# A gated-convolution and retention block on one Trainium2 core: the first head's v and gate computed plain, q and k between the quads, one convolution slice between two heads, stores on POOL's queue

## The chip, the cores and the metric

The kernel runs on one core of a Trainium2 chip. The metric is the device time of one execution, in microseconds. A core has a matrix engine (TensorE, "PE" in the profile, with its weight loads as "PEld"), a vector engine (VectorE, "DVE"), a scalar engine (ScalarE, "ACT"), a general engine (GpSimd, "POOL") and a queue engine (SyncE, "SP") from which most DMAs are issued. POOL can issue DMAs too. Each engine works through its own list of instructions in order; semaphores hold an instruction back until what it needs is there. On-chip memory has 128 partitions; matmul results go to eight accumulator banks of 128 x 512 numbers.

## The reference

One layer on x of 512 tokens by 1024 features, in float32:

```python
h    = rmsnorm(x, g_mix)
proj = h @ w_in            # conv x | B | C | q | k | v | swish gate | gate A | gate R
u    = gc * xc
y_a  = (gb * depthwise_conv3(u)) @ w_a_out
# 4 heads, q and k 256 wide with rotary, v 512 wide
ret  = retention(q, k, v, gamma_f) + retention_backward(q, k, v, gamma_b)
y_r  = (groupnorm_per_head(ret) * g_ret * silu(g_sw)) @ w_r_out
x    = x + (sigmoid(gate_a) * y_a + sigmoid(gate_r) * y_r) @ w_o
h2   = rmsnorm(x, g_ffn)
x    = x + (silu(h2 @ w_ff_gate) * (h2 @ w_ff_up)) @ w_ff_down
out  = rmsnorm(x, g_final)
```

The normalisation is a gain per feature times one number per token (1/rms), so a projection can be made from x with the gain alone, and each token's result scaled by 1/rms afterwards.

## The kernel before

Every float32 matmul is done as three matmuls of operands split into a high and a low part (`mm3`, lines 272 to 276): high times high, high times low, low times high. `split` (line 158) makes the two parts: ACT writes the high part (line 161 or 164) and DVE the low part (line 162 or 165).

Weights stream in from memory in the order of the list that `plan()` writes out (line 54). There are two kinds of entries. A "c" entry is a block of 1 MB, loaded by SP in pieces (line 198) and split into two units; `feature_major` (line 282) turns a block of 8 x 128 rows and 256 columns into two banks with features on partitions, and `token_major` (line 299) turns blocks of 4 x 128 rows and 512 columns into four banks with tokens on partitions. A "q" entry is one of seven weight forms of a Strassen product ("quad"): four quarter matrices are loaded (line 222), four of the seven forms are sums of two quarters made by DVE (line 234), and `strassen` (line 340) replaces eight products by seven. One quad yields two 512-column outputs, for example v and the swish gate of a head. Weight units are kept in five buffers, so splits run up to two and a half blocks ahead; `raw` has ten buffers for what is loaded and not yet split.

The work in order:

1. x arrives in four loads of 512 KB beside the first weight block and is split with the gain into `xu` (line 395). `SumSq` squares x (line 419), adds up, and gives 1/rms per token (`rstd_tokens`, with a pow on POOL at line 442) and as a row along the free axis (`rstd_row`).
2. `do_qk(0)` computes q and k of head 0 from the unnormalised `xu`, with 1/rms worked into the rotary table `rcs`. Then x is normalised (line 552), split into `xg`, and its four sums for Strassen are made and split (lines 567 and 569). `do_qk(1)` to `do_qk(3)` follow, from `xu`. Each rotates on DVE (lines 539 to 541) and splits and stores the result (`keep`, line 518) in DRAM from SP. `decays()` (line 488) makes the four decay tables.
3. Four quads give v and gate of the heads, two more the merge gates A and R. Results are stored from SP (lines 585 and 591).
4. `do_mix(s)` for four slices of the convolution: three weight blocks each, a product and a three-tap convolution on DVE, result z split and stored.
5. The retention, head by head: `load_head` reads q, k, the table, v and gate back; `do_scores` makes the decayed scores p; `split_v` splits v; `do_pv` multiplies p by v and applies the group norm (statistics on DVE at line 668, a pow on POOL at line 671, then lines 673 and 675); `do_t` transposes on DVE (line 175) and splits; `do_wr` multiplies by w_r_out. Its first head stores to `yrd` from SP (line 690), the next two add to it with accumulating DMAs from POOL (line 692), and the last adds in on-chip memory. The mixes 0 to 2 come before head 0's scores, mix 3 after them.
6. `ysum` (the sum in `yrd`), the gates `sgr` and z are loaded, in this order, from SP (line 629); then `do_wr(3)`, `do_wa`, the output projection and the feed-forward part, which the change doesn't touch.

512-column scratch tiles (`t512`, lines 152 and 153) have nine buffers, the large tiles (`big`) fourteen, and the tiles for `rcs`, the decay tables and the convolution's u two. The order of instructions on each engine is fixed when the kernel is built, by a scheduler that lets later instructions go ahead where they are ready and buffers are free.

Of the kernel before, what the change touches and what calls it, by code (L numbers as in the profile page):

```python
# [12 lines left out]
F32 = mybir.dt.float32  # L13
F32R = mybir.dt.float32r
AF = mybir.ActivationFunctionType
ALU = mybir.AluOpType
# [37 lines left out]
def plan():  # L54

    out = []  # L60

    def a(name, col):
        out.append(("c", name, 0, 8, col, 256))

    def b(name, row, nk, col, nc):
        out.append(("c", name, row, nk, col, nc))

    def quad(c0, c1):
        for name in FORMS:
            for u in (0, 2):  # L70
                out.append(("q", ("w", c0, c1), name, u, 2))

    for h in range(HEADS):
        a("w_in", C_Q + h * QK)
        a("w_in", C_K + h * QK)
    for h in range(HEADS):
        quad(C_V + h * VD, C_G + h * VD)
    for c in (0, 512):
        quad(C_GA + c, C_GR + c)
    for s in range(4):  # L80
        for c in (C_XC, C_GC, C_GB):
            a("w_in", c + s * 256)
    for h in range(HEADS):
        for c in (0, 512):
            b("w_r_out", h * VD, 4, c, 512)
    for c in (0, 512):
        for r in (0, 512):
            b("w_a_out", r, 4, c, 512)
    for r in (0, 512):
        for c in (0, 512):  # L90
            b("w_o", r, 4, c, 512)
    def f(q, *names):
        for n in names:
            out.append(("q", ("f", q), n, 0, 4))

    f(0, "b11", "b21", "b12", "b22")
    f(1, "b11", "b21")
    for q0, n in FF_PARTS:
        for q in range(max(q0, 1), q0 + n):
            f(q, "t1", "t2", "t3")  # L100
            if q + 1 < NQ:
                f(q + 1, "b11")
            f(q, "t4")
            if q + 1 < NQ:
                f(q + 1, "b21")
# [27 lines left out]
def block_kernel(ctx: ExitStack, tc: tile.TileContext, xT, xtok, wpack, wquad, cols, decs, rot, g_ffn, g_final, out):  # L133
# [21 lines left out]
    def bank():  # L155
        return psum.tile([P, 512], F32, tag="bank", name="bank")
# [121 lines left out]
    def act_pair(tiles, k, sl=slice(0, S)):  # L278
        hi, lo = tiles
        return hi[k // 4][:, k % 4, sl], lo[k // 4][:, k % 4, sl]  # L280

    def feature_major(rhs, evict, block0=0, row_first=False):

        c = Chunk()
        if row_first:
            pss = [bank(), bank()]
            for k in range(8):
                for m in range(2):
                    mm3(pss[m], c.w(k, m * P, P), act_pair(rhs, k), k == 0, k == 7)
            for m in range(2):  # L290
                evict(block0 + m, pss[m])
            return
        for m in range(2):
            ps = bank()
            for k in range(8):
                mm3(ps, c.w(k, m * P, P), act_pair(rhs, k), k == 0, k == 7)
            evict(block0 + m, ps)

    def token_major(lhs, row0, chunks, evict):

        pss = [bank() for _ in range(NB)]
        n = 4 * chunks
        for kk in range(n):
            if kk % 4 == 0:
                c = Chunk()
            for nb in range(NB):
                mm3(pss[nb], act_pair(lhs, row0 + kk, slice(nb * P, (nb + 1) * P)),
                    c.w(kk % 4, 0, 512), kk == 0, kk == n - 1)
        for nb in range(NB):
            evict(nb, pss[nb])  # L310
# [85 lines left out]
        split(xs[k // 4][:, k % 4, :], xu[0][k // 4][:, k % 4, :], xu[1][k // 4][:, k % 4, :],  # L396
              gmix[:, k:k + 1])

    def split_two(c):
        split_x(2 * c)  # L400
        split_x(2 * c + 1)
    prefetch(4, lambda c: load_x(2 * c, 2), split_two)
    rcs = misctile(D, "rcs").rearrange("p (i n) -> p i n", i=2)
    prefetch(2)
    nc.sync.dma_start(rcs, rot)
# [112 lines left out]
    def keep(dst, src):  # L518
        hi, lo = t512(F32R), t512(F32R)
        split(src, hi, lo)  # L520
        for d, t in zip(dst, (hi, lo)):
            nc.sync.dma_start(d, t.bitcast(F32))


    def do_qk(h):
        pss = []
        for j in range(2):
            feature_major(xu, lambda m, ps: pss.append(ps), row_first=h == 0 and j == 0)
            if h == 0 and j == 0:
                ss.rstd_tokens()  # L530
        if h == 0:
            nc.scalar.copy(rrow, ss.rstd_row())
            for i in range(2):
                nc.vector.tensor_tensor(out=rcs[:, i, :], in0=rcs[:, i, :], in1=rrow, op=ALU.mult)
        cos, sin = rcs[:, 0, :], rcs[:, 1, :]
        for j in range(2):
            for i, (c1, c2, op) in enumerate(((cos, sin, ALU.subtract), (sin, cos, ALU.add))):
                a, b = t512(), t512()
                nc.vector.tensor_tensor(out=a, in0=pss[2 * j], in1=c1, op=ALU.mult)  # L539
                nc.vector.tensor_tensor(out=b, in0=pss[2 * j + 1], in1=c2, op=ALU.mult)  # L540
                nc.vector.tensor_tensor(out=a, in0=a, in1=b, op=op)
                keep([t[:, 2 * j + i, :] for t in qkd[h]], a)

    rrow = t512()
    do_qk(0)

# [25 lines left out]
    xforms = {n: of(t) for n, t in sums(*(xs[i][:, :, o:o + 256] for o in (0, 256) for i in range(2))).items()}  # L572
    for n, i, o in (("a11", 0, 0), ("a12", 1, 0), ("a22", 1, 256)):
        xforms[n] = of((xg[0][i], xg[1][i]), o)
    for h in range(1, HEADS):
        do_qk(h)
    decays()


    def do_quad(left, right, func, func_left=None):  # L580
        def ev_sum(dst, o, f):
            def ev(tt, t):
                if f:
                    nc.scalar.activation(t, t, f)
                nc.sync.dma_start(dst[:, o + tt, :], t)
            return ev

        def ev21(tt, ps):
            t = t512()
            nc.scalar.activation(t, ps, func_left or AF.Copy)  # L590
            nc.sync.dma_start(left[:, 2 + tt, :], t)
        strassen(4, xforms, ev_sum(left, 0, func_left), ev21, ev_sum(right, 2, func), ev_sum(right, 0, func))

    for h in range(HEADS):
        do_quad(vd[h], sgd[h], AF.Silu)
    for j in range(2):
        do_quad(gad[j], grd[j], AF.Sigmoid, AF.Sigmoid)


    def do_mix(s):  # L600
# [84 lines left out]
    def do_wr(h, yr):  # L685
        for half in range(2):
            def ev(nb, ps):
                t = snap(ps)
                if h == 0:
                    nc.sync.dma_start(yrd[half][:, nb, :], t)  # L690
                else:
                    nc.gpsimd.dma_start(out=yrd[half][:, nb, :], in_=t, accum_op=ALU.add)

            def ev_last(nb, ps):
                t = ysum[half][:, nb, :]
                nc.vector.tensor_tensor(out=t, in0=ps, in1=t, op=ALU.add)
                nc.vector.tensor_tensor(out=t, in0=t, in1=sgr[half][:, nb, :], op=ALU.mult)
            token_major(yr, 0, 1, ev if h < HEADS - 1 else ev_last)

    do_mix(0)  # L700
    do_mix(1)
    do_mix(2)
    qk, tab, v, sg = load_head(0)
    p = do_scores(qk, tab)
    vv = split_v(v)
    do_mix(3)
    yr = None
    for h in range(HEADS):
        if h < HEADS - 1:
            nxt = load_head(h + 1)  # L710
        do_pv(p, vv, sg)
        if h < HEADS - 1:
            p = do_scores(nxt[0], nxt[1])
        if yr:
            new = do_t(h, sg)
            do_wr(h - 1, yr)
            yr = new
        else:
            yr = do_t(h, sg)
        if h < HEADS - 1:  # L720
            vv, sg = split_v(nxt[2]), nxt[3]


    ysum = [load(t) for t in yrd]
    sgr = [load(t) for t in grd]
    z = [[load(t, F32R) for t in x] for x in zd]
    do_wr(HEADS - 1, yr)
    sga = [load(t) for t in gad]
    mt = ([], [])
# [272 lines left out]
    def store(nb, scaled=()):  # L1002
# [28 lines left out]

    def ev_a(tt):
        to_y(a[tt], 2 + tt, 0, last=True)
        store(2 + tt)

    def ev_d(tt):
        to_y(d[tt], tt, 1, last=True)
        store(tt, (0,) if tt else ())
    prod_tm(n, forms["a22"], a, False, True, ev_a)
    prod_tm(n, forms["s4"], d, False, True, ev_d)  # L1040

# [64 lines left out]
```

## Time and profile before

| | |
|---|---|
| runs | 1101.33, 1101.3 and 1100.21 us; median 1101.3 us |
| the profiled execution | 1101.26 us |
| its span in the profile | 1099.5 us |
| mean granted clock of TensorE | 0.98 |
| moved by DMA | 177.11 MB, mean 161 GB/s |
| PEld busy | 898.4 us |

The profile gives the busy time of each engine, the same in forty equal slices, the chain of work that ended last, groups of instructions by line with their mean duration, and the DMA issues with the time to landing. The trace behind it can be asked who waited for whom, what an engine did in a stretch, and for the single instructions in order of time. Matmuls overlap, so PE's busy time is not a count of work: the number of matmuls in a stretch is.

### The profile page before, as it was taken

Reading aid. Unit: us, or ns where it says so; the run is one execution under the profiler, and the core shown is the slowest. Engines: PE = TensorE matmul, PEld = TensorE weight load, DVE = VectorE, ACT = ScalarE, POOL = GpSimd, SP = SyncE. Lnnn points to the kernel's source line nnn. Section 1 sums busy time; section 2 is a strip of 40 time slices with the busy share of each in tenths; the row PEclk is TensorE's granted clock in tenths of the full one; section 3 lists DMA queues with packets and bytes.
Section 4 is the critical chain, followed back from the end, with each engine's and each line's share of the span. In section 5 each row is a group of like instructions: output and inputs, shape, how many; then the busy total and the mean of one; then the engine's idle time right before and its main releaser. Section 6 shows DMA issues by size and latency. Waiting matters only on the chain.

```text
span 1099.5 us, 14236 instructions
## 1 busy us (share of the span) xinstructions
PE 1050.2 (96%) x5448; PEld 898.4 (82%) x5448; DVE 841.8 (77%) x1087; ACT 496.5 (45%) x667; POOL 51.8 (5%) x70
## 2 busy tenths in 40 slices
PE   7999799999999999993999979999999999999996
PEld 6878588888888888882888868889997999899985
DVE  7899987797684444568889844448988898979995
ACT  6434375556655232322235311235555555545653
POOL 1000000000000000000002200000001000010001
PEclk9999899999999999996999999999999999999999
DMA  9446675434546424744176596442116632472313
GB/s 341 166 138 217 220 263 216 160 140 179 192 152 213 149 105 145 268 148 169 58 268 137 124 310 271 175 141 68 59 58 177 172 104 85 122 185 95 137 20 95
DMA packets 57683, 177.11 MB, mean 161 GB/s; under 512 B 6544, under 2 KB 6544, under 8 KB 54288
## 3 DMA queue, kind: packets, MB, share of 16 engines
q1 hardware_dynamic: 52432, 166.78, 42.2%
q0 software_dynamic: 5184, 9.44, 5.7%
q8 instruction: 42, 0.69, 0.2%
q14 instruction: 25, 0.20, 0.1%
HBM read 134.51 MB, written 41.68 MB: 160 GB/s over the span
## 4 chain that ended last, share of the span: by engine, by line
PE 79%; DVE 15%; issue 2%; DMA 1%; ACT 1%; POOL 1%; SPq 0%; POOLq 0%; ACTq 0%; DVEq 0%
PE bank L330 28%; PE bank L836 20%; PE bank L274 10%; PE bank L275 10%; PE bank L276 10%; DVE big L175 3%; DVE wlo L162 2%; DVE big L162 1%; DMA big<-z 1%; DVE t L162 1%; DVE big L675 1%; DVE bnst L668 1%; DVE t L673 1%; POOL bnmv L671 1%; DVE t L539 1%
## 5 line engine op out<-in xcount | busy, mean ns | idle before, releaser
L162 DVE TENSOR_TENSOR wlo<-raw,whi 128x1024 fp32r<-128x1024 f32 (+1 forms) x272 | 323.7, 1198 | 162.1 <-ACT whi L161 160.0
L161 ACT CAST whi<-raw 128x1024 fp32r<-128x1024 f32 (+1 forms) x272 | 279.9, 1033 | 331.8 <-PE bank L276 86.5
L836 PE MATMUL bank<-xform,whi 128*128 128x256 f32 x1248 | 227.8, 284 | 0.0
L836 PEld LDWEIGHTS bank<-xform,whi 128*128 128x128 f32 x1248 | 194.8, 192 | 2.9 <-ACT t L929 1.6
L330 PE MATMUL bank<-whi,big 128*128 128x512 f32 x596 | 187.4, 390 | 0.4 <-DVE big L1026 0.3
L836 PE MATMUL bank<-xform,wlo 128*128 128x256 f32 x624 | 175.4, 283 | 0.0
L234 DVE TENSOR_TENSOR raw<-raw 128x1024 f32<-128x1024 f32 x112 | 132.7, 1199 | 2.4 <-DMA raw<-wquad 1.5
L330 PEld LDWEIGHTS bank<-whi,big 128*128 128x128 f32 x596 | 111.7, 188 | 25.6 <-ACT t L337 0.8
L274 PE MATMUL bank<-big,whi 128*128 128x512 f32 x320 | 126.8, 397 | 4.0 <-ACT big L164 4.0
L276 PE MATMUL bank<-big,wlo 128*128 128x512 f32 x320 | 126.8, 396 | 2.0 <-DVE wlo L162 2.0
L275 PE MATMUL bank<-big,whi 128*128 128x512 f32 x320 | 126.7, 396 | 0.0
L330 PE MATMUL bank<-whi,xform 128*128 128x512 f32 x384 | 122.9, 396 | 1.2 <-ACT whi L161 1.2
L836 PEld LDWEIGHTS bank<-xform,wlo 128*128 128x128 f32 x624 | 119.2, 192 | 0.0
L330 PE MATMUL bank<-wlo,big 128*128 128x512 f32 x298 | 116.0, 390 | 1.4 <-DVE wlo L162 1.4
L274 PE MATMUL bank<-whi,big 128*128 128x512 f32 x240 | 95.1, 399 | 5.6 <-DMA big<-z 5.6
L275 PE MATMUL bank<-wlo,big 128*128 128x512 f32 x240 | 94.4, 393 | 0.0
L276 PE MATMUL bank<-whi,big 128*128 128x512 f32 x240 | 92.6, 390 | 0.0
L330 PEld LDWEIGHTS bank<-whi,xform 128*128 128x128 f32 x384 | 73.3, 191 | 17.4 <-ACT whi L161 2.1
L330 PE MATMUL bank<-wlo,xform 128*128 128x512 f32 x192 | 76.4, 398 | 4.4 <-DVE wlo L162 4.4
L274 PEld LDWEIGHTS bank<-big,whi 128*128 128x128 f32 x320 | 61.3, 192 | 17.1 <-ACT big L164 4.3
L276 PEld LDWEIGHTS bank<-big,wlo 128*128 128x128 f32 x320 | 61.4, 192 | 15.3 <-DVE wlo L162 2.4
L275 PEld LDWEIGHTS bank<-big,whi 128*128 128x128 f32 x320 | 61.2, 191 | 13.3 <-DVE big L165 0.4
(145 smaller groups left out, 1180.8 us busy)
## 6 DMA issues: line engine op xcount, KB each, us to landing
raw<-wquad SPq DMA_DIRECT2D x112, 512.0 KB, 4.1
raw<-wpack SPq DMA_DIRECT2D x70, 512.0 KB, 4.4
qh<-t SPq DMA_DIRECT2D x16, 256.0 KB, 2.5
ql<-t SPq DMA_DIRECT2D x16, 256.0 KB, 2.5
big<-qh SPq DMA_DIRECT2D x4, 1024.0 KB, 7.2
big<-ql SPq DMA_DIRECT2D x4, 1024.0 KB, 8.7
v<-t SPq DMA_DIRECT2D x16, 256.0 KB, 2.5
sg<-t SPq DMA_DIRECT2D x16, 256.0 KB, 3.0
```

The costliest lines, as they stand in the source:

```text
L161: nc.scalar.copy(hi, src)
L162: nc.vector.tensor_tensor(out=lo, in0=src, in1=hi.bitcast(F32), op=ALU.subtract)
L175: nc.vector.transpose(o[:, :, :, b, :], i[:, :, :, q, :])
L234: nc.vector.tensor_tensor(out=t, in0=t, in1=raws[quad, more, u][:, 0:n], op=ALU.add)
L274: nc.tensor.matmul(ps, lh, rh, start=first, stop=False)
L275: nc.tensor.matmul(ps, lh, rl, start=False, stop=False)
L276: nc.tensor.matmul(ps, ll, rh, start=False, stop=last)
L330: nc.tensor.matmul(pss[tt], l, r[:, c], start=start and k == 0 and i == 0, stop=stop and k == n - 1 and i == 2, skip_group_check=True)
L539: nc.vector.tensor_tensor(out=a, in0=pss[2 * j], in1=c1, op=ALU.mult)
L668: nc.vector.bn_stats(st, ps)
L671: nc.gpsimd.tensor_tensor(out=mv[:, 3:4], in0=mv[:, 2:3], in1=mhalf[:, 0:1], op=ALU.pow)
L836: nc.tensor.matmul(o, l[:, c], r[:, k], start=start and s == 0 and k == 0 and i == 0, stop=stop and k == 3 and i == 2, skip_group_check=True)
```

## The change

- Head 0's v and gate are no longer made by a quad but as plain token-major products from the unnormalised `xu`, first of all; 1/rms per token scales the results on their way out of the banks (ACT). The 1/rms matmuls come before the last eighth of v's product (`before_v`), the row of 1/rms after v.
- q and k of each head come from the normalised `xg`, right behind that head's v and gate; the rotary table keeps its values. `decays()` moves behind the last gate quad. x comes in four loads of 256 KB and two of 512 KB.
- `do_mix(3)` moves from before the heads to between heads 0 and 1; head 0's scores and v split come ahead of `do_mix(2)` instead of `do_mix(3)`. In each head the next head's `split_v` comes before `do_t` instead of at the end.
- z and `sgr` are loaded before `do_wr(2)`; `ysum` is loaded from POOL's queue.
- The stores of q, k, v, gates, z and of the first `yrd` are issued from POOL instead of SP.

```diff
--- before.py
+++ after.py
@@ plan
+    for c in (C_V, C_G):
+        for r in (0, 512):
+            b("w_in", r, 4, c, 512)
     for h in range(HEADS):
+        if h:
+            quad(C_V + h * VD, C_G + h * VD)
         a("w_in", C_Q + h * QK)
         a("w_in", C_K + h * QK)
-    for h in range(HEADS):
-        quad(C_V + h * VD, C_G + h * VD)
...
-    def token_major(lhs, row0, chunks, evict):
+    def token_major(lhs, row0, chunks, evict, before=None):
...
+            if before:
+                before(kk)
...
-    prefetch(4, lambda c: load_x(2 * c, 2), split_two)
+    prefetch(4, load_x, split_x)
+    for k in (4, 6):
+        load_x(k, 2)
+    for k in range(4, 8):
+        split_x(k)
...
-            nc.sync.dma_start(d, t.bitcast(F32))
...
-    rrow = t512()
-    do_qk(0)
+            store(d, t.bitcast(F32))
+
+    def store(dst, t):
+        nc.gpsimd.dma_start(dst, t)
+
+    def before_v(kk):
+        if kk == 7:
+            rtok.append(ss.rstd_tokens())
+    rtok = []
+    for dst, func in ((vd[0], AF.Copy), (sgd[0], AF.Silu)):
+        def ev(nb, ps):
+            t = t512()
+            nc.scalar.activation(t, ps, func, scale=rtok[0][:, nb:nb + 1])
+            store(dst[:, nb, :], t)
+        token_major(xu, 0, 2, ev, None if rtok else before_v)
+        if func == AF.Copy:
+            rrow = snap(ss.rstd_row())
...
-    for h in range(1, HEADS):
-        do_qk(h)
-    decays()
+    def do_qk(h):
+        for j in range(2):
+            pss = []
+            feature_major(xg, lambda m, ps: pss.append(ps))
+            cos, sin = rcs[:, 0, :], rcs[:, 1, :]
+            for i, (c1, c2, op) in enumerate(((cos, sin, ALU.subtract), (sin, cos, ALU.add))):
+                a, b = t512(), t512()
+                nc.vector.tensor_tensor(out=a, in0=pss[0], in1=c1, op=ALU.mult)
+                nc.vector.tensor_tensor(out=b, in0=pss[1], in1=c2, op=ALU.mult)
+                nc.vector.tensor_tensor(out=a, in0=a, in1=b, op=op)
+                keep([t[:, 2 * j + i, :] for t in qkd[h]], a)
...
     for h in range(HEADS):
-        do_quad(vd[h], sgd[h], AF.Silu)
+        if h:
+            do_quad(vd[h], sgd[h], AF.Silu)
+        do_qk(h)
     for j in range(2):
         do_quad(gad[j], grd[j], AF.Sigmoid, AF.Sigmoid)
+    decays()
...
     do_mix(0)
     do_mix(1)
+    nxt = load_head(0)
+    p = do_scores(nxt[0], nxt[1])
+    vv, sg = split_v(nxt[2]), nxt[3]
     do_mix(2)
-    qk, tab, v, sg = load_head(0)
-    p = do_scores(qk, tab)
-    vv = split_v(v)
-    do_mix(3)
     yr = None
     for h in range(HEADS):
         if h < HEADS - 1:
             nxt = load_head(h + 1)
         do_pv(p, vv, sg)
+        t = sg
         if h < HEADS - 1:
             p = do_scores(nxt[0], nxt[1])
-        if yr:
-            new = do_t(h, sg)
+            vv, sg = split_v(nxt[2]), nxt[3]
+        new = do_t(h, t)
+        if h == 0:
+            do_mix(3)
+        else:
+            if h == HEADS - 1:
+                z = [[load(t, F32R) for t in x] for x in zd]
+                sgr = [load(t) for t in grd]
             do_wr(h - 1, yr)
-            yr = new
-        else:
-            yr = do_t(h, sg)
-        if h < HEADS - 1:
-            vv, sg = split_v(nxt[2]), nxt[3]
-
-    ysum = [load(t) for t in yrd]
-    sgr = [load(t) for t in grd]
-    z = [[load(t, F32R) for t in x] for x in zd]
+        yr = new
+
+    ysum = [bigtile(), bigtile()]
+    for t, d in zip(ysum, yrd):
+        nc.gpsimd.dma_start(t, d)
     do_wr(HEADS - 1, yr)
```

The stores at lines 585, 591 and 690 become calls of `store` as well, and the final output's function of that name is renamed.

More of the change, by code (lines that the diff above doesn't have):

```diff
@@ L280, in act_pair, with feature_major @@
         return hi[k // 4][:, k % 4, sl], lo[k // 4][:, k % 4, sl]
-    def feature_major(rhs, evict, block0=0, row_first=False):
+    def feature_major(rhs, evict, block0=0):
         c = Chunk()
[L285 to L292, printed above, removed]
         for m in range(2):
@@ L397, in split_x @@
               gmix[:, k:k + 1])
-    def split_two(c):
-        split_x(2 * c)
-        split_x(2 * c + 1)
-    prefetch(4, lambda c: load_x(2 * c, 2), split_two)
+    prefetch(4, load_x, split_x)
[3 more added lines that the diff above has]
+        split_x(k)
     rcs = misctile(D, "rcs").rearrange("p (i n) -> p i n", i=2)
@@ L521, in keep @@
         for d, t in zip(dst, (hi, lo)):
-            nc.sync.dma_start(d, t.bitcast(F32))
[L525 to L542, printed above, removed]
-    rrow = t512()
-    do_qk(0)
+            store(d, t.bitcast(F32))
[13 more added lines that the diff above has]
+            rrow = snap(ss.rstd_row())
     xg = quarters()
@@ L584, in ev @@
                     nc.scalar.activation(t, t, f)
-                nc.sync.dma_start(dst[:, o + tt, :], t)
+                store(dst[:, o + tt, :], t)
             return ev
@@ L590, in ev21 @@
             nc.scalar.activation(t, ps, func_left or AF.Copy)
-            nc.sync.dma_start(left[:, 2 + tt, :], t)
+            store(left[:, 2 + tt, :], t)
         strassen(4, xforms, ev_sum(left, 0, func_left), ev21, ev_sum(right, 2, func), ev_sum(right, 0, func))
     for h in range(HEADS):
-        do_quad(vd[h], sgd[h], AF.Silu)
+        if h:
+            do_quad(vd[h], sgd[h], AF.Silu)
+        do_qk(h)
     for j in range(2):
         do_quad(gad[j], grd[j], AF.Sigmoid, AF.Sigmoid)
+    decays()
     def do_mix(s):
@@ L689, in ev @@
                 if h == 0:
-                    nc.sync.dma_start(yrd[half][:, nb, :], t)
+                    store(yrd[half][:, nb, :], t)
                 else:
@@ L1000, in gain, with put @@
         nc.vector.tensor_tensor(out=yt, in0=yt, in1=gf[:, half * 512:(half + 1) * 512], op=ALU.mult)
-    def store(nb, scaled=()):
+    def put(nb, scaled=()):
         for half in (1, 0):
@@ L1033, in ev_a @@
         to_y(a[tt], 2 + tt, 0, last=True)
-        store(2 + tt)
+        put(2 + tt)
     def ev_d(tt):
         to_y(d[tt], tt, 1, last=True)
-        store(tt, (0,) if tt else ())
+        put(tt, (0,) if tt else ())
     prod_tm(n, forms["a22"], a, False, True, ev_a)
```

## The prediction

> **What bounds the kernel now.** I read the page's busy times first, then the waits of PE, then PE's busy time and matmul count stretch by stretch, then the timeline, the groups and the DMA issues at the holes.
>
> ```profile
> span 1099.5 us, 14236 instructions
> PE 1050.2 (96%) x5448; PEld 898.4 (82%) x5448; DVE 841.8 (77%) x1087; ACT 496.5 (45%) x667; POOL 51.8 (5%) x70
> PE   7999799999999999993999979999999999999996
> ```
>
> TensorE (PE) is the bound: 96% of the span, with holes near the start, near 510 us (the 3), near 650 us and at the end. The second view is who PE waited for.
>
> ```profile
> PE bank L274 <- ACT big L161: 19.0, 1, 19.0
> PE bank L330 <- DVE wlo L162: 5.8, 3, 2.8
> PE bank L274 <- DMA big<-z: 5.6, 1, 5.6
> PE bank L274 <- ACT big L164: 4.0, 1, 4.0
> PE bank L276 <- DVE wlo L162: 2.0, 1, 2.0
> ```
>
> Columns: total us, times, longest. Busy time counts a matmul as long at half clock as an idle array, so I count matmuls in stretches instead (the number behind PE's busy time; GB/s last, granted clock third from the end).
>
> ```profile
> 0.00:140.00 140.00, 125.84 (x511) 101.29 (x512) 124.91 (x190) 63.65 (x83) 5.78 (x10) 0.95 0.60 217
> 140.00:340.00 200.00, 200.00 (x884) 165.62 (x883) 155.64 (x152) 118.46 (x146) 0.00 (x0) 1.00 0.53 187
> 340.00:480.00 140.00, 140.00 (x620) 115.91 (x619) 66.10 (x88) 46.77 (x58) 0.00 (x0) 1.00 0.50 174
> 480.00:540.00 60.00, 41.00 (x170) 32.98 (x169) 48.21 (x81) 10.65 (x17) 4.36 (x8) 0.83 0.28 105
> 640.00:680.00 40.00, 34.42 (x142) 27.94 (x141) 15.96 (x21) 6.32 (x6) 0.00 (x0) 0.91 0.86 334
> 60.00:80.00 20.00, 17.98 (x72) 14.38 (x71) 20.00 (x23) 8.37 (x9) 0.88 (x1) 0.91 0.39 128
> ```
>
> From 140 to 340 us PE never stops: 884 matmuls of 512 columns in 200 us, 0.2262 us each. With that price:
> - 0 to 140: 511 less 16 warm-up and 8 two-column ones is 487, worth 110.2 us; **29.8 us lost**.
> - 480 to 540: 170, worth 38.5; **21.5 lost**.
> - 640 to 680: 142, worth 32.1; **7.9 lost**.
>
> A stop costs more than its wait: between 60 and 80 us 72 matmuls are worth 16.3, so 3.7 were lost, though the one wait there is the 2.0 on L276; the clock was 0.91 in that stretch. I call the other 1.7 us the restart.
>
> **Part 1, v and gate of head 0 plain.** The Strassen quad is 7 products of 4 k, 2 tiles, 3 matmuls: 168. Plain, two outputs of 8 k, 4 token blocks, 3 matmuls: 192. 24 more at 0.2262 is **+5.4 us**, certain.
>
> **Part 2, the first 140 us.** Now four q/k heads (DVE rotation, hi/lo split, decay tables, forms of x) stand before any quad, and DVE is the late one: 20.00 of 20 us busy in the last row above. After, v and gate (192 matmuls, 43.4 us) need from DVE only splits and the normalised x, and each later head pairs 168 + 96 matmuls = 59.7 us of PE.
>
> ```profile
> L162 DVE TENSOR_TENSOR wlo<-raw,whi 128x1024 fp32r<-128x1024 f32 x261 | 316.6, 1220 | 158.0 <-ACT whi L161 155.9 <-DMA z<-t 1.6
> L234 DVE TENSOR_TENSOR raw<-raw 128x1024 f32<-128x1024 f32 x108 | 130.2, 1218 | 2.4 <-DMA raw<-wquad 1.5
> L539 DVE TENSOR_TENSOR t<-bank,rcs 128x512 f32<-128x512 f32 x16 | 10.9, 680 | 0.0
> L552 DVE SCALAR_TENSOR_TENSOR big<-big,cols_sb,t 128x512 f32<-128x512 f32 x8 | 5.7, 737 | 0.0
> L161 ACT CAST t<-t 128x512 fp32r<-128x512 f32 x26 | 16.1, 618 | 54.3 <-DVE t L541 21.6 <-DVE t L622 18.8 <-DVE lw L478 5.6
> 6.51 1.15 ACT L419 ACTIVATE t<-big 128x512 f32<-128x512 f32 x2 [1.43 <-DMA big<-xT]
> 8.85 1.22 PE L274 MATMUL bank<-big,whi 128*128 128x512 f32 x2 [4.01 <-ACT big L164]
> 13.72 0.41 PE L276 MATMUL bank<-big,wlo 128*128 128x512 f32 x1
> 25.49 0.27 PE L436 MATMUL bank<-ones_r,t 128*128 128x2 f32 x1 [1.05 <-DVE t L162]
> 26.30 0.49 PE L274 MATMUL bank<-big,whi 128*128 128x512 f32 x1
> 26.94 1.99 POOL L442 TENSOR_TENSOR rtok<-rtokv,mhalf 128x4 f32<-128x4 f32 x1 [3.44 <-DVE lw L473]
> ```
>
> DVE per later head: 14 weight splits and 8 sums of a quad, 22 x 1.22 = 26.8; six evictions, 4.1; rotation and split, 16 x 0.68 = 10.9; four q/k weight splits, 4.9. Together 46.7 of 59.7 us, so it is hidden; without the pairing it would be a q/k head's 15.8 in 21.7 plus the forms, which is today's jam. While the gate's 96 matmuls (21.7 us) run, DVE must finish the 8 x 0.737 = 5.9, four x splits of 1.2 and four weight splits, 15.7 in all; the forms' 4 sums and 4 splits, 8 x 1.22 = 9.8, then fall under q0 and k0 (21.7 us, beside 10.9 of rotation: here DVE is tight).
>
> What remains lost: the first matmul comes at 8.85 because ACT squared the first 512 KB of x at 6.51; x now comes in blocks of 256 KB, and I take 7.5 (bounds 6.5 and 8.85). The half clock after it: the 11 matmuls before 13.72 us would take 2.5, not 4.9, so 2.4. Seven of the eight small matmuls took 0.8 (25.49 to 26.30), so 1.0. The new weak place is the joint between v and gate: the small matmuls come before the last 12 of v (2.7 us), while the pow behind them took 1.99, then a split (0.62 on ACT, 0.68 on DVE) before the two matmuls for the row of 1/rms, behind which the gate's matmuls are queued on PE. About 1.3 us late plus the restart of 1.7: 3.0 (bounds 0 and two such stops of 3.7). 7.5 + 2.4 + 1.0 + 3.0 = 13.9, so **-15.9 us** (bounds -19.9 and -10.1).
>
> **Part 3, mix(3) between heads 0 and 1, split_v before do_t.** The 19.0 wait is head 1's v split (L161 on ACT), queued behind head 0's norms, scores and transposes.
>
> ```profile
> 501.58 0.69 DVE L175 STREAM_TRANSPOSE big<-big 32x512 f32<-32x512 f32 x1
> 502.86 10.73 DVE L175 STREAM_TRANSPOSE big<-big 32x512 f32<-32x512 f32 x15
> 517.18 1.22 PE L274 MATMUL bank<-big 128*128 128x512 f32 x2 [18.96 <-ACT big L161]
> 485.00:523.00 38.00, 19.00 (x73) 14.76 (x72) 30.45 (x50) 6.92 (x10) 2.19 (x4) 0.73 0.38 144
> ```
>
> mix(3) is 3 x 48 = 144 matmuls, 32.6 us, more than the hole. But it brings DVE work: the mixes between 340 and 480 us had 66.10 us of DVE per 620 matmuls, 15.4 for 144. DVE then has 30.45 + 15.4 = 45.8 in a stretch where PE has (73 + 144) x 0.2262 = 49.1: it fits, closely. What is late next is the weight split of mix(3)'s last block, behind 11.4 us of transposes. I leave one stop of 0.9 and a restart: **-18.9 us** of 21.5 (bounds -21.5 and -11; the latter leaves a block of transposes uncovered). mix(2) takes mix(3)'s place over the split of head 0's scores, with the same 144 matmuls.
>
> **Part 4, z and gate loads ahead of do_wr(2), ysum on POOL's queue.**
>
> ```profile
> 644.79 0.33 SPq L629 DMA_DIRECT2D big<-yr  x1
> 645.21 0.86 SPq L629 DMA_DIRECT2D big<-gr  x2
> 646.16 2.23 SPq L629 DMA_DIRECT2D big<-z  x4
> big<-z SPq DMA_DIRECT2D x4, 1024.0 KB, 13.6
> ```
>
> SP's queue stood until 644.79 at the load of the sum that the accumulates write; z, queued behind, landed 13.6 us after issue. After, z issues once head 3's tiles come free, and do_wr(2) and do_wr(3) (192 matmuls, 43.4 us) cover 13.6 three times. ysum, now behind the accumulates on POOL, is read by evictions only, with four other banks free for PE. **-7.9 us** (bounds -7.9 and 0).
>
> **Part 5, stores on POOL's queue.** 32 for q/k, 16 each for v, gate and z, 16 for the two merge gates, 8 for yr: 104. SP issues none of them; the trace has no plain store on POOL, the nearest rows are its accumulates.
>
> ```profile
> L692 POOL DMA_DIRECT2D yr<-t x16 | 14.5, 1321 | 33.9 <-ACT t L337 33.9
> L946 POOL DMA_DIRECT2D ydr<-t x16 | 14.1, 965 | 204.3 <-DVE t L348 164.6 <-DVE t L356 27.4 <-DVE t L363 6.3
> yr<-t POOLq DMA_DIRECT2D x16, 256.0 KB, 7.2
> qh<-t SPq DMA_DIRECT2D x16, 256.0 KB, 2.5
> L671 POOL TENSOR_TENSOR bnmv<-bnmv,mhalf 128x1 f32<-128x1 f32 x16 | 8.7, 544 | 504.8 <-DVE bnmv L670 504.8
> ```
>
> At 0.97 to 1.32 us each POOL issues for 101 to 137 us of some 650, where it is idle now. Two things can bite: the pows of L671, for which DVE and then PE's banks wait, queue behind stores; and each store holds one of nine 512-column tiles for up to 7.2 instead of 2.5 us, so that a rotation (four tiles a pass) waits for one. A head's slack on DVE (59.7 - 46.7 = 13.0) covers four passes of 3.3 us. Earlier loads on SP could give a little back (bound -1). I take **+2 us**, nearer to nothing, since accumulates ahead of pows already occur for heads 2 and 3 without a PE stop; upper bound in the last rival.
>
> The Trainium skill ("SBUF — State Buffer", SBUF: two separate sides, and Who interferes with whom) speaks against the move: while DVE runs an operation that takes both its ports, such as an fp32 copy, GpSimd cannot write the descriptors of a DMA issued from its queue. By it stores would stall wherever DVE copies; this kernel's DVE work is nearly all tensor_tensor, which the page excludes, so by the rule the sum would not change, and no run here shows a stall of that kind.
>
> **Sum.** 5.4 - 15.9 - 18.9 - 7.9 + 2.0 = -35.3. The profiled execution took 1101.26 us, 1.8 more than its span and equal to the median of 1101.3, so **1066**.
>
> **Rivals.**
> - *The early jam stays* (chance 0.13): DVE is still the late engine because x's forms, rotation and quad 1's splits meet at its start. For it: DVE's 124.91 us of 140. Against: the first head's quad is gone with its 26.8 us. Part 2 gives nothing: 1066 + 15.9 = 1082.
> - *The hole moves behind mix(3)* (0.11): DVE's 45.8 of 49.1 cannot be packed, and pv(1) or the next weights come a transpose block late. 11.4 us less 2.6 already counted: 1066 + 9 = 1075.
> - *z is as late as before* (0.06): its loads wait for big tiles that head 3 still holds, or block the weights behind them on SP. Then the change doesn't do what it says here: 1066 + 7.9 = 1074. Against: 43 us of cover.
> - *Slower: the nine tiles run dry* (0.09). 24 passes of rotation and convolution end in two stores. If each pass waits for both to land, 7.2 + 2 x 0.97 = 9.1 us, a q/k head's four passes cost 36.6 less 13.0 of slack, 23.6; four heads 94, less 35.3: 1101 + 59 = 1160. It decides from (35.3 / 4 + 13.0) / 4 = 5.5 us of wait a pass. Against: nine tiles hold two passes, and the banks leave half a head between the pairs.
>
> **How the numbers follow.** Forecast 0.60, with its own range 1058 to 1072; rivals as given; 0.01 for losses that just eat the gain. The three milder rivals lie within 1082. All bounds at their best give 5.4 - 19.9 - 21.5 - 7.9 - 1 = -44.9, 1056; above, the early jam and some of a second rival reach 1085. Outside remain about 0.15. Faster by over 0.2% (about what a measurement of this kernel can tell from no change): 0.60 + 0.13 + 0.11 + 0.06 = 0.90; within it 0.01; slower 0.09.
>
> **What would show it.** Part 1: matmuls on PE up by 24. Part 2: no PE wait on wlo L162 between 40 and 140 us, and at most one stop near 30. Part 3: no long PE wait on a v split; instead mix(3)'s matmuls behind head 1's scores. Part 4: no PE wait for the z load. Part 5: POOL busy for 100 us or more, pows not over 1 us later. I am wrong if PE stops more than 15 us in all between 10 and 700 us, above all on splits that wait for a tile still being stored by POOL.

## The result

The changed kernel takes 1061.45 us (median of 4 runs, 1061.35 to 1061.88) against 1100.88 us (4 runs, 1100.21 to 1101.33): a ratio of 0.9643, 95% interval 0.9626 to 0.966. The forecast was 1066 us with a range of 1056 to 1085. The profiled execution of the changed kernel took 1061.37 us.

### The profile page after: what moved, and what is told of

It is laid out like the page before. It is cut to its first block, busy times and chain, and to the rows that moved or that the text cites. A ratio compares the mean times of both kernels' runs of the same rounds, so it can differ in the third digit from the quotient of the medians.

```text
span 1059.6 us, 14292 instructions
## 1 busy us (share of the span) xinstructions
PE 1042.1 (98%) x5472; PEld 895.3 (84%) x5472; DVE 821.6 (78%) x1065; ACT 494.3 (47%) x663; POOL 108.2 (10%) x176
## 4 chain that ended last, share of the span: by engine, by line
PE 88%; DMA 4%; DVE 4%; issue 2%; ACT 1%; POOL 1%; SPq 0%; POOLq 0%; DVEq 0%; ACTq 0%
PE bank L328 26%; PE bank L842 21%; PE bank L277 13%; PE bank L279 13%; PE bank L278 13%; DMA big<-yr 2%; DMA yr<-t 1%; DMA big<-xT 1%; DMA tab<-tab 1%; DVE wlo L165 1%; DVE big L1014 0%; DVE t L423 0%; PE bank L801 0%; PE bank L751 0%; ACT whi L164 0%
## 5 line engine op out<-in xcount | busy, mean ns | idle before, releaser
L165 DVE TENSOR_TENSOR wlo<-raw,whi 128x1024 fp32r<-128x1024 f32 (+1 forms) x266 | 316.7, 1199 | 149.8 <-ACT whi L164 147.3
L164 ACT CAST whi<-raw 128x1024 fp32r<-128x1024 f32 (+1 forms) x266 | 273.5, 1033 | 315.5 <-PE bank L279 81.3
L328 PE MATMUL bank<-whi,big 128*128 128x512 f32 x548 | 172.5, 391 | 1.5 <-ACT t L335 1.2
L237 DVE TENSOR_TENSOR raw<-raw 128x1024 f32<-128x1024 f32 x104 | 123.7, 1199 | 1.5 <-DMA raw<-wquad 0.8
L277 PE MATMUL bank<-big,whi 128*128 128x512 f32 x320 | 124.5, 389 | 0.0
L278 PE MATMUL bank<-big,whi 128*128 128x512 f32 x320 | 124.5, 389 | 0.0
L279 PE MATMUL bank<-big,wlo 128*128 128x512 f32 x320 | 124.5, 389 | 0.0
L328 PEld LDWEIGHTS bank<-whi,big 128*128 128x128 f32 x548 | 102.7, 188 | 25.3 <-ACT t L335 2.4
L277 PE MATMUL bank<-whi,big 128*128 128x512 f32 x304 | 119.4, 395 | 4.1 <-ACT big L167 1.9
L278 PE MATMUL bank<-wlo,big 128*128 128x512 f32 x304 | 119.1, 392 | 0.0
L279 PE MATMUL bank<-whi,big 128*128 128x512 f32 x304 | 118.5, 392 | 0.0
L328 PE MATMUL bank<-wlo,big 128*128 128x512 f32 x274 | 106.7, 390 | 1.4 <-DVE wlo L165 1.4
L328 PE MATMUL bank<-whi,xform 128*128 128x512 f32 x320 | 100.1, 389 | 0.0
L277 PEld LDWEIGHTS bank<-whi,big 128*128 128x128 f32 x304 | 57.4, 189 | 18.0 <-ACT big L167 2.2
L277 PEld LDWEIGHTS bank<-big,whi 128*128 128x128 f32 x320 | 60.1, 188 | 12.6
L328 PEld LDWEIGHTS bank<-whi,xform 128*128 128x128 f32 x320 | 60.1, 188 | 12.5
```

The source lines that it names most:

```text
L164: nc.scalar.copy(hi, src)
L165: nc.vector.tensor_tensor(out=lo, in0=src, in1=hi.bitcast(F32), op=ALU.subtract)
L237: nc.vector.tensor_tensor(out=t, in0=t, in1=raws[quad, more, u][:, 0:n], op=ALU.add)
L277: nc.tensor.matmul(ps, lh, rh, start=first, stop=False)
L278: nc.tensor.matmul(ps, lh, rl, start=False, stop=False)
L279: nc.tensor.matmul(ps, ll, rh, start=False, stop=last)
```

## The profile after

The page first: the span, the busy engines, and PE in forty slices.

```profile
span 1059.6 us, 14292 instructions
PE 1042.1 (98%) x5472; PEld 895.3 (84%) x5472; DVE 821.6 (78%) x1065; ACT 494.3 (47%) x663; POOL 108.2 (10%) x176
PE   8999999999999999999999999999999999999996
```

PE has 24 matmuls more (5472 against 5448) and 8 us less of busy time: less of it is spent at a lowered clock (mean granted clock 0.997, where it was 0.98). The hole of the 19th slice is gone. POOL went from 52 to 108 us. Who PE still waits for:

```profile
PE bank L277 <- ACT big L167: 1.9, 1, 1.9
PE bank L277 <- ACT whi L164: 1.4, 1, 1.4
PE bank L328 <- DVE wlo L165: 1.4, 1, 1.4
PE bank L328 <- ACT t L335: 1.2, 1, 1.2
PE bank L374 <- DVE lw L467: 1.1, 1, 1.1
PE bank L452 <- ACT t L164: 0.9, 1, 0.9
PE bank L277 <- DVE big L700: 0.7, 1, 0.7
```

The same stretches as before the change (the number behind PE's time is its matmuls):

```profile
0.00:140.00 140.00, 134.84 (x587) 110.94 (x588) 117.69 (x167) 82.09 (x102) 19.74 (x38) 0.99 0.67 243
480.00:540.00 60.00, 60.00 (x266) 49.71 (x265) 51.52 (x82) 18.91 (x27) 10.94 (x20) 1.00 0.71 252
540.00:640.00 100.00, 97.86 (x430) 80.36 (x429) 73.88 (x104) 33.04 (x45) 17.65 (x22) 1.00 0.74 227
```

PE's stop at the joint between v and gate, where line 452 makes the row of 1/rms:

```profile
32.39 0.50 PE L452 MATMUL bank<-t,ones_r 128*128 128x512 f32 x1 [0.95 <-ACT t L164]
```

At the 0.2262 us of the prediction, 0 to 140 holds 587 - 24 = 563 matmuls, 127.4 us, so 12.6 are lost where 29.8 were: 17.2 gained. The stretch round 510 us lost 21.5 and loses nothing. Between 540 and 640 us 430 matmuls are worth 97.3, so 2.7 are lost there. Its two stops lie at 618 and 621 us, where line 700 reads the sum of the heads on DVE:

```profile
617.67 1.29 DVE L700 TENSOR_TENSOR big<-bank,big 128x512 f32<-128x512 f32 x2 [9.16 <-DMA big<-yr]
618.46 0.47 PE L277 MATMUL bank<-whi,big 128*128 128x512 f32 x1 [1.42 <-ACT whi L164]
620.81 0.50 PE L277 MATMUL bank<-whi,big 128*128 128x512 f32 x1 [0.72 <-DVE big L700]
```

DVE waited 9.16 us for the load of the sum. The profile puts the first stop down to a weight split on ACT, but that split had ended at 618.12; PE went on 0.1 us after the first addition of line 700 (617.67 and 0.68), as it did at the second stop. I read both as waits for line 700 to free a bank. Before, the same work lost 7.9 behind the z load, and 0.7 in the 100 us ahead of it. That makes 17.2 + 21.5 + 5.9 - 5.4 = 39.2, and the spans differ by 39.9.

Two groups of instructions of the changed kernel follow, the stores of q's high part on POOL and the step of the group norm behind the pow:

```profile
L524 POOL DMA_DIRECT2D qh<-t x16 | 8.7, 546 | 87.5 <-ACT t L164 84.1 <-ACT t L335 3.4
L677 DVE TENSOR_SCALAR t<-bank,bnmv 128x512 f32<-128x512 f32 x16 | 13.0, 810 | 11.4 <-POOL bnmv L675 11.4
```

The same step in the kernel before:

```profile
L673 DVE TENSOR_SCALAR t<-bank,bnmv 128x512 f32<-128x512 f32 x16 | 12.9, 809 | 11.3 <-POOL bnmv L671 11.3
```

And the DMA issues of three groups of stores in the changed kernel (count, KB each, median us to landing):

```profile
qh<-t POOLq DMA_DIRECT2D x16, 256.0 KB, 2.6
v<-t POOLq DMA_DIRECT2D x16, 256.0 KB, 5.3
ga<-t POOLq DMA_DIRECT2D x8, 256.0 KB, 5.8
```

A plain store costs POOL 0.55 us, about half of an accumulate, and lands 2.6 to 5.8 us after issue, by what is stored. DVE waits 11.4 us in all for the pows of the group norm, against 11.3 before, so the stores don't hold the pows up.

## The experiments

Each kernel is the changed one with the edit shown, except the ninth. The first four ran on one chip, the next four on a second, the last four on a third; the kernel before took 1101.1, 1098.1 and 1097.0 us on these, the changed kernel itself 1061.68 us on the third. On the second the changed kernel wasn't run; the kernel with seven scratch tiles, which differs from it in nothing else, took 1061.74 us there.

### The stores back on SP

```diff
-        nc.gpsimd.dma_start(dst, t)
+        nc.sync.dma_start(dst, t)
```

> The changed kernel with all its plain stores issued from SP again instead of POOL; nothing else differs. Theory A (the move to POOL's queue costs and brings nothing, since POOL is idle and SP's queue has slack): 1061 us, within 2 us of the changed kernel. Theory B (stores on SP hold up the weight loads queued behind them): PE stops on weight splits in the quads, 1064 to 1075 us. Theory C (POOL's stores hold scratch tiles too long): faster than the changed kernel by 2 us or more.

Measured: 1061.22 us (1060.04 to 1061.51), ratio 0.9644 (0.9628 to 0.9661), the same as with POOL. The DMA issues of this kernel:

```profile
qh<-t SPq DMA_DIRECT2D x16, 256.0 KB, 2.4
v<-t SPq DMA_DIRECT2D x16, 256.0 KB, 3.6
ga<-t SPq DMA_DIRECT2D x8, 256.0 KB, 3.1
```

The plain stores land 2.3 to 3.6 us after issue from SP, where POOL's took 2.6 to 5.8: the high part of q hardly differs, v and gate A land 1.7 and 2.7 us later from POOL. The time doesn't show it, so theory A holds: moving the stores neither costs nor brings anything here.

### The convolution slice back ahead of the heads, the v split still early

```diff
     do_mix(2)
+    do_mix(3)
     yr = None
...
-        if h == 0:
-            do_mix(3)
-        else:
+        if h:
```

> The changed kernel with the fourth convolution slice back ahead of the heads, but the next head's v split still ahead of the transposes. Theory A (two causes made the hole of 21.5 us: the order on DVE and the lack of PE work): the v split comes before 11.4 us of transposes, so the hole shrinks to about 7 us plus a restart of 1.7, and the time is about 1070 us. Theory B (only the lack of PE work matters): the whole hole returns, about 1083 us. Theory C (only the order matters): no hole, 1061 us.

Measured: 1075.18 us, ratio 0.9774 (0.9757 to 0.979): 13.7 of the 21.5 us return, more than theory A said and less than B. PE's longest wait in this kernel:

```profile
PE bank L277 <- DVE t L677: 10.2, 1, 10.2
```

DVE in order of time ahead of that wait's end (start, duration):

```profile
493.34 11.44 DVE L178 STREAM_TRANSPOSE big<-big 32x512 f32<-32x512 f32 x16
504.82 1.29 DVE L672 BATCH_NORM_STATS2 bnst<-bank 128x6 f32<-128x512 f32 x2
```

With v split early, PE goes on to head 1's product, but its four banks wait for the group norm (statistics at line 672, then line 677), which DVE reaches only after the 11.44 us of transposes. The block of transposes is the obstacle whichever step is behind it; moving one step ahead of it hands the wait to the next.

### Both back: slice ahead, v split behind the transposes

```diff
     do_mix(2)
+    do_mix(3)
     yr = None
...
-            vv, sg = split_v(nxt[2]), nxt[3]
         new = do_t(h, t)
...
         yr = new
+        if h < HEADS - 1:
+            vv, sg = split_v(nxt[2]), nxt[3]
```

> The changed kernel with the fourth convolution slice ahead of the heads and the v split behind the transposes, as before the change; all else as changed. By the count of lost matmuls the hole of 21.5 us returns: 1083 us, with one PE wait of about 19 us on the v split. If the gain of this part had come from elsewhere (loads, stores): clearly less, under 1075 us.

Measured: 1083.01 us, ratio 0.9845 (0.9829 to 0.9861), with the old wait, to the tenth:

```profile
PE bank L277 <- ACT big L164: 19.0, 1, 19.0
```

So this part is worth 21.6 us. The early v split alone is worth 7.8 of them, and the slice behind it the rest. The slice with a late v split was not run.

### z and the merge gate behind the sum, on SP

```diff
-            if h == HEADS - 1:
-                z = [[load(t, F32R) for t in x] for x in zd]
-                sgr = [load(t) for t in grd]
...
-    ysum = [bigtile(), bigtile()]
-    for t, d in zip(ysum, yrd):
-        nc.gpsimd.dma_start(t, d)
+    ysum = [load(t) for t in yrd]
+    sgr = [load(t) for t in grd]
+    z = [[load(t, F32R) for t in x] for x in zd]
```

> The changed kernel with the loads of z and of the merge gate behind those of the sum, all on SP, as before the change. Theory A: the PE wait for z of 5.6 us and its restart return, while the stops of 2.1 us that the changed kernel has there go: 1061 + 7.9 - 2.7 = 1066 us. Theory B (the weights were what was late): no change, 1061 us.

Measured: 1068.01 us (1066.82 to 1069.26), ratio 0.971 (0.9688 to 0.9732). PE's longest wait:

```profile
PE bank L277 <- DMA big<-z: 6.4, 1, 6.4
```

SP's issues in order of time:

```profile
610.99 0.33 SPq L633 DMA_DIRECT2D big<-yr  x1
611.41 0.86 SPq L633 DMA_DIRECT2D big<-gr  x2
612.36 2.15 SPq L633 DMA_DIRECT2D big<-z  x4
```

The z loads again leave only after the sum's second half, and PE waits for them. Theory A holds, 2 us dearer than expected. (The edit also takes the sum's load from POOL back to SP.)

### q and k of all heads in one stretch

```diff
     for h in range(HEADS):
-        if h:
-            do_quad(vd[h], sgd[h], AF.Silu)
         do_qk(h)
+    for h in range(1, HEADS):
+        do_quad(vd[h], sgd[h], AF.Silu)
```

(with the weights' list in the same order)

> The changed kernel with q and k of all four heads in one stretch behind head 0's v and gate, then the three quads. Theory A (it is the pairing of q/k with quads that gives DVE room): DVE has about 83 us of work in the 87 us of the four q/k heads, with the decay tables on top, and PE stops on weight splits as before the change: 6 to 12 us lost, 1067 to 1073 us. Theory B (the plain v and gate ahead are enough, since they cover the normalisation of x): 1061 to 1064 us.

Measured: 1060.00 us (1059.64 to 1061.46), ratio 0.9651 (0.9631 to 0.9671). Theory A falls: no jam returns. The first 140 us of this kernel:

```profile
0.00:140.00 140.00, 134.69 (x592) 110.17 (x593) 116.16 (x177) 68.34 (x87) 23.55 (x45) 1.00 0.70 254
```

592 matmuls, against 583 to 591 in the ten profiles with the pairing and with v and gate plain ahead; the first product came at 5.62 us here and at 6.77 us in the changed kernel (587), which is five matmuls. So by this count it is no better and no worse than with the pairing. DVE is busy for 116.16 us, 9 less than before the change, while PE does 81 matmuls more.

### Head 3's v and gate plain too

```diff
-        if h:
-            quad(C_V + h * VD, C_G + h * VD)
+        if h == 3:
+            for c in (C_V, C_G):
+                for r in (0, 512):
+                    b("w_in", r, 4, c + h * VD, 512)
+        elif h:
+            quad(C_V + h * VD, C_G + h * VD)
...
+        if h == 3:
+            for dst, func in ((vd[h], AF.Copy), (sgd[h], AF.Silu)):
+                def ev3(nb, ps):
+                    t = t512()
+                    nc.scalar.activation(t, ps, func)
+                    store(dst[:, nb, :], t)
+                token_major(xg, 0, 2, ev3)
```

> The changed kernel with head 3's v and gate plain as well, from the normalised x. Theory A (a plain pair costs its 24 more matmuls and DVE's relief of 17 us buys nothing where PE doesn't stop): 1061.4 + 5.4 = 1066.9 us. Theory B (DVE's relief is worth something in the quads): 1063 us or less.

Measured: 1067.2 us (1066.68 to 1067.46), ratio 0.9712 (0.9697 to 0.9728): 5.8 more than the changed kernel's 1061.45, and 5.5 more than the kernel with seven tiles on the same chip, so theory A. Where PE never stops, a plain pair costs its 24 matmuls (5.4 us), and DVE's relief buys nothing:

```profile
140.00:340.00 200.00, 200.00 (x884) 165.61 (x883) 127.84 (x137) 93.05 (x116) 27.10 (x50) 1.00 0.51 179
```

The same stretch of the changed kernel:

```profile
140.00:340.00 200.00, 200.00 (x884) 165.62 (x883) 148.64 (x158) 103.41 (x129) 28.17 (x52) 1.00 0.54 186
```

PE runs 884 matmuls in these 200 us in both, with DVE busy for 127.84 us instead of 148.64.

### Seven scratch tiles instead of nine

```diff
-    tmp = ctx.enter_context(tc.tile_pool(name="tmp", bufs=9))
+    tmp = ctx.enter_context(tc.tile_pool(name="tmp", bufs=7))
```

> The changed kernel with seven scratch tiles of 512 columns instead of nine. Theory A (stores from POOL land about as soon as from SP, so that tiles are plentiful): within 2 us of 1061 us. Theory B (nine is close to the edge, and the stores' longer hold would tell with seven): 1066 us or more, with DVE or ACT waiting for stores.

Measured: 1061.74 us (1059.92 to 1062.3), ratio 0.966 (0.9643 to 0.9678): no change. Nine tiles are not near an edge.

### Heads 2 and 3 added up in the banks

```diff
+    def do_wr_pair(y0, y1):
+        pss = [[bank() for _ in range(NB)] for _ in range(2)]
+        for i, y in enumerate((y0, y1)):
+            for half in range(2):
+                c = Chunk()
+                for k in range(4):
+                    for nb in range(NB):
+                        mm3(pss[half][nb], act_pair(y, k, slice(nb * P, (nb + 1) * P)), c.w(k, 0, 512),
+                            i == 0 and k == 0, i == 1 and k == 3)
...
+                ysum = [load(t) for t in yrd]
+                do_wr_pair(yr, new)
```

(behind the second head, each half goes through the two operations of `ev_last`; the loads of z and the merge gate stay ahead)

> The changed kernel with the products of heads 2 and 3 by w_r_out added up in the same eight banks, so that only head 1's go through an accumulating DMA and the sum is loaded long before it is read. Theory A (the two stops of 2.1 us near 620 us come from the sum, which is loaded late behind the accumulates): they go, with a restart, and the time is 1058 to 1059 us. Theory B (they come from the weight split or the z load): they stay, 1061 us.

Measured: 1058.99 us (1058.65 to 1059.28), ratio 0.9638 (0.9623 to 0.9653). The stretch that lost 2.7 us:

```profile
540.00:640.00 100.00, 100.00 (x443) 82.81 (x442) 76.29 (x108) 29.66 (x38) 9.74 (x13) 1.00 0.63 211
```

443 matmuls, no loss. Theory A: those stops came from the sum's way through memory. The size is read from the times and the count: 2.8 us less than the kernel with seven tiles on the same chip, and 13 matmuls (2.9 us) more than the changed kernel's 430. The ratio alone (0.9638 against 0.9643) would not show it, since the kernel before was faster on this chip.

### The pairing alone, in the kernel before

```diff
     for h in range(HEADS):
         a("w_in", C_Q + h * QK)
         a("w_in", C_K + h * QK)
-    for h in range(HEADS):
         quad(C_V + h * VD, C_G + h * VD)
...
-    for h in range(1, HEADS):
-        do_qk(h)
-    decays()
...
     for h in range(HEADS):
+        if h:
+            do_qk(h)
         do_quad(vd[h], sgd[h], AF.Silu)
     for j in range(2):
         do_quad(gad[j], grd[j], AF.Sigmoid, AF.Sigmoid)
+    decays()
```

> The kernel before with one thing of the change alone: q and k of each later head behind the quad of the head ahead of it, and the decay tables behind the gate quads. Head 0's q and k still come first from the unnormalised x, head 0's v and gate are still a quad. Theory C (what takes the jam away is plain v and gate ahead, with 17 us less on DVE and 43 us of PE work that needs no normalised x): quad 0 now needs the normalised x and its sums as early as 36 us, when DVE is some 15 to 20 us behind, so PE stops there instead: 1095 to 1106 us. Theory A of the prediction (the pairing gives DVE its room): most of 17 us gained, 1083 to 1090 us.

Measured: 1112.1 us, ratio 1.0127 (1.011 to 1.0144): slower than the kernel before, by 15.1 us on its chip and by more than theory C allowed. PE's waits in this kernel:

```profile
PE bank L329 <- ACT big L160: 16.0, 2, 9.4
PE bank L273 <- ACT big L163: 8.1, 1, 8.1
```

The stretch from 20 to 60 us, where the kernel before has 166 matmuls:

```profile
20.00:60.00 40.00, 22.57 (x94) 17.56 (x93) 37.05 (x77) 15.61 (x20) 5.21 (x2) 0.80 0.32 121
```

Its first product in order of time:

```profile
12.91 1.22 PE L273 MATMUL bank<-big,whi 128*128 128x512 f32 x2 [8.07 <-ACT big L163]
```

The 16.0 us in two waits for the split of the normalised x, between 40 and 58 us, are what theory C said. A side effect adds to them: the loads run a fixed number of list entries ahead, quad 0 now stands third in the list, and its quarters were loaded ahead of the first weights and x, so the first product came at 12.91 instead of 8.85 us. SP's first issues of this kernel (`wquad` holds the quad's quarters, `wpack` the other weights):

```profile
0.74 1.34 SPq L221 DMA_DIRECT2D raw<-wquad  x3
2.13 0.43 SPq L197 DMA_DIRECT2D raw<-wpack  x1
```

So the 15.1 us are not the price of the pairing by itself; theory A, which wanted 1083 to 1090 us, fails by more than this side effect of 4 us.

### Three edits together

The pair of the eighth kernel, the order of the fifth, and

```diff
-        if kk == 7:
+        if kk == 6:
```

> The changed kernel with three edits: heads 2 and 3 added up in the banks, the 1/rms matmuls one step earlier in v, and q and k of all heads in one stretch. Theory: the stops near 620 us (2.1 and a restart), near 32 us (1 to 2 and a restart) and near 106 us (1.2 and a restart, from the decay tables' exponentials among a quad's evictions) go: 1056 us where the changed kernel takes 1061. Rival: the earlier 1/rms matmuls wait for the sum of squares instead, and only the stops near 620 and 106 us go: 1058 us.

Measured: 1055.73 us (1055.63 to 1056.63), ratio 0.9617 (0.96 to 0.9633), 6.0 less than the changed kernel on the same chip.

```profile
0.00:140.00 140.00, 136.09 (x595) 111.03 (x596) 116.70 (x177) 68.97 (x87) 23.78 (x46) 1.00 0.70 255
540.00:640.00 100.00, 100.00 (x443) 82.83 (x442) 76.70 (x110) 29.56 (x38) 9.34 (x12) 1.00 0.63 211
```

595 and 443 matmuls; the changed kernel on this chip has 583 and 432, and 23 matmuls are 5.2 us. The forecast of 1056 holds, but not each step of it. The stops near 620 and 106 us are gone. Near 32 us two waits stand at the 1/rms matmuls, the first of them for the sum of squares, as the rival said:

```profile
PE bank L435 <- DVE t L165: 0.5, 1, 0.5
PE bank L453 <- DVE t L165: 0.3, 1, 0.3
```

The changed kernel has one of 0.4 us there on this chip, so the third edit shows no gain of its own. And the first product came at 5.76 us, against 6.74 us for the changed kernel beside it; none of the edits touches that, and in all profiles with x in blocks of 256 KB it lies between 5.6 and 6.9 us.

### x in four loads of 512 KB

```diff
-    prefetch(4, load_x, split_x)
-    for k in (4, 6):
-        load_x(k, 2)
+    prefetch(4, lambda c: load_x(2 * c, 2), split_x)
```

> The changed kernel with x in four loads of 512 KB as before the change. Theory: the first matmul waits for 512 KB and for ACT behind it, 8.5 to 9 us instead of 6.8: 1063 to 1064 us. Rival (the start is hidden by later slack, or the first matmul waits for the weights): 1061 us.

Measured: 1062.41 us (1062.09 to 1062.62), ratio 0.9675 (0.9659 to 0.9692), 0.7 more than the changed kernel beside it. Its first product:

```profile
8.73 0.80 PE L277 MATMUL bank<-whi,big 128*128 128x512 f32 x1 [3.96 <-ACT big L167]
```

Its first 140 us:

```profile
0.00:140.00 140.00, 134.88 (x584) 111.62 (x585) 118.06 (x167) 82.06 (x102) 20.15 (x38) 0.98 0.65 243
```

The first product of the changed kernel on this chip:

```profile
6.74 0.79 PE L277 MATMUL bank<-whi,big 128*128 128x512 f32 x1 [1.89 <-ACT big L167]
```

And its first 140 us:

```profile
0.00:140.00 140.00, 135.08 (x583) 111.13 (x584) 116.47 (x166) 81.79 (x102) 19.66 (x38) 1.00 0.66 240
```

The start is 2.0 us later, as the theory said, but the time lies below the 1063 to 1064 us of the theory and above the rival's 1061. By 140 us as many matmuls are done: this kernel has no stop near 32 and 106 us, which the changed one has. So most of the 2 us was paid back at later joints; why the stops are not there, these two traces don't show.

### The changed kernel again

No edit.

> The changed kernel itself, on the same chip as the three others, so that differences of 1 to 3 us can be read: 0.9643 of the kernel before.

Measured: 1061.68 us (1060.91 to 1061.94), ratio 0.9667 (0.965 to 0.9683); the kernel before was 0.35% faster here than in the result above, the changed one was not, so ratios taken on different chips can differ by 0.25% though the kernels are the same.

## Why the prediction was right, point by point

- **Part 1, +5.4 us.** Right: 24 more matmuls, and a second plain pair cost 5.5 to 5.8 us.
- **Part 2, -15.9 us.** The size was right (-17.2), one reason was wrong. The prediction held that without the pairing of q/k and quads DVE would fall back into "today's jam". With q and k in one stretch there is no jam (1060.00 us), and the pairing alone, put into the kernel before, made it slower (1112.1 us, some of it from loads that it put ahead of x). That leaves the plain v and gate at the head: 43 us of PE work that asks little of DVE and nothing of the normalised x. This is by elimination: the stores, the size of x's loads and the pairing were tried alone, q and k from the normalised x and the place of the tables were not, and no run separates the lighter load on DVE from the early place of this work. The weak joint between v and gate was there, with a wait of 0.95 us where 1.3 was estimated, but no restart of 1.7 followed: the clock was 1.00 from 20 to 60 us, and the stop cost some 1.2 us where the sum had 3.0. Not in the sum was a stop of 1.2 us near 106 us, told below, which cost about 1.4. So it is partly luck that 12.6 us lost came so near to the 13.9 forecast: one term too large met one that was missing.
- **Part 3, -18.9 us.** Right in mechanism, the size too small by 2.6: no stop is left, and undoing it costs 21.6 us. DVE's 45.8 of 49.1 could be packed, without the stop of 0.9 and the restart that the prediction left there.
- **Part 4, -7.9 us.** Half a miss in size: -5.9 in the count, 6.6 when undone. z is on time, as said. The step that failed is that the sum "is read by evictions only", with four other banks free: the four banks of `do_wr(3)`'s second half hold 48 matmuls, 10.9 us of cover, and the first half of the sum, issued at 601.50 us, landed 16.1 us later, when both halves of the product were done. PE stopped twice behind line 700, for 1.42 and 0.72 us, and 2.7 us were lost. Adding up two heads in the banks removes them.
- **Part 5, +2 us.** The true size is 0 within what the runs can tell (1061.22 with SP). The upper bound was taken from accumulates (0.97 to 1.32 us to issue, 7.2 to land); a plain store takes 0.55 and 2.6 to 5.8. Even with seven tiles the time is the same, so the slower rival had no ground.
- **The sum.** -35.3 against -39.4 measured: parts 2, 3 and 5 were 1.3, 2.6 and 2.0 better, part 4 was 2.0 worse. Between 10 and 700 us PE's stops come to 4.3 us, where the prediction had set 15 as the sign of being wrong.

## What to carry to other kernels

Count matmuls per stretch instead of busy time, and price each hole by the matmuls that are missing from it: three holes priced so gave the result within 5 us, with some luck in the first. When a hole is one engine's block of work (here 11.4 us of transposes), bringing one step ahead of it wins only a part (7.8 of 21.6 us) and hands the wait to the next step; independent work for the waiting engine closes it. And test a plausible cause by itself: the pairing looked like the reason for the early gain, was not needed for it, and without the rest of the change made things worse.

## What the runs showed of the hardware that was not expected

- A plain store of 256 KB issued from POOL occupies it for 0.55 us and lands in 2.6 to 5.8 us, where the same stores from SP land in 2.3 to 3.6; accumulates of the same size occupy POOL for 0.97 to 1.35 us and land in 6 to 10.
- Not every stop of PE has a restart. In the kernel before, the 2.02 us of waiting that ended at 73.75 us were followed, from 75.27 us on, by eight matmuls in 3.4 us, at about half the pace of the others; this is what the prediction called the restart. The stops of 0.7 to 1.4 us in the changed kernel have nothing of the kind, and neither has one of 2.12 us, ended at 33.00 us, in the kernel with q and k in one stretch. What decides it, no run here shows.
- Written last, the decay tables were built between 63 and 131 us all the same, in gaps on DVE. Their exponentials fell among a quad's silu evictions, and ACT reloaded its function table between the two kinds: these two lines have seven loads of 1.28 us in the changed kernel, three where q and k come in one stretch. Two groups of the changed kernel:

```profile
L585 ACT ACT_TABLE_LOAD x4 | 5.1, 1283 | 0.1
L500 ACT ACT_TABLE_LOAD x3 | 3.8, 1283 | 1.9 <-DVE scr L499 1.9
```

PE's stop behind ACT, and ACT ahead of it, in order of time:

```profile
105.26 0.95 ACT L500 ACTIVATE tab<-scr 128x896 f32<-128x896 f32 x1 [1.78 <-DVE scr L499]
106.12 0.57 ACT L335 COPY t<-bank 128x512 f32<-128x512 f32 x1
106.71 1.28 ACT L585 ACT_TABLE_LOAD   x1
106.74 0.50 PE L328 MATMUL bank<-whi,big 128*128 128x512 f32 x1 [1.17 <-ACT t L335]
```

The copy of line 335 frees PE's bank. It stood on ACT behind an exponential that had itself waited 1.78 us for DVE; the table load comes only after the copy. So this stop comes from the order of instructions on ACT, and not from a table load.
